# Value products of a half as one run, and norm roots on VectorE, in a two-layer hybrid encoder

## The chip, the cores and the metric

The kernel runs on one core of one Trainium2 chip. The metric is the device time of one execution in microseconds (us). Three executions of the kernel before took 1064.05 to 1065.41 us, with a median of 1065.24 us.

## The reference

The input is a sequence of 512 positions of 1024 channels (float32). Two layers follow each other. Each layer has a mixing part and a convolutional feed-forward part. Cut to what matters here, the mixing part is:

```python
h = rmsnorm(x, norm1[l]);  p = h @ w_in[l]          # columns: u (512) | q (8x64) | k (2x64) | v (2x64)
y_f = Re(fft2(u)) @ w_f + b_f                       # Fourier half
q = rope(rmsnorm(q, q_norm[l]))                     # each head of 64 is normed on its own
k = rope(rmsnorm(k, k_norm[l]))
# windowed attention: queries in 4 blocks of 128, keys of the own block and its two neighbours,
# |i - j| <= 128, a learned sink logit per head; 4 query heads share one key and value head
probs = softmax(concat([q @ k.T / 8, sink]))[..., :-1]
y_a = probs @ v
x = x + concat([rmsnorm(y_f), rmsnorm(y_a)]) @ w_o[l]
```

The feed-forward part is `x = x + (silu(g) * u) @ w_down` with `[g, u] = dwconv3(rmsnorm(x) @ w_up)`. It takes most of the time and is not touched by the change.

## The kernel before

Activations are kept transposed (channels on the partitions), and most products of float32 operands are made as three products of float32r parts: each operand is split into a rounded high part and a low rest (`split`, lines 98 to 105), and `mm3` (lines 114 to 122) accumulates high by high, low by high and high by low. A few products, the value products among them, are made on plain float32 operands; each of these is two MATMUL records in the trace.

A layer runs in these stages. The combined projection is made first for the columns of k, v and one pair of q heads, then for the rest (lines 373 to 396). `fold_h` (line 400) makes the folded inputs of the Fourier half on VectorE and ScalarE. `prep` (line 429) squares q or k on ScalarE, sums each head on VectorE, takes the inverse root with `rsqrt` (line 206), and applies norm scale and rotary tables on VectorE; it is called for k with q pair 3 (16 roots a partition) and later for q pairs 0 to 2 (24 roots a partition). `turn_k` and `turn_q` transpose the results on TensorE. Then come the two Fourier stages (line 594), with attention of pair 3 written between them and of pair 0 behind them, the product with `w_f` (line 622), the attention of pairs 1 and 2, and the output projection: its Fourier half (line 669) first, which is the fill for the attention of pairs 1 and 2, and its attention half (line 676) after it.

`attention(p, ...)` (line 500) handles one pair of heads in two halves of two query blocks each. For each block and head it makes the scores (line 517, PSUM tag `sc`), adds the mask and takes the extremum on VectorE (line 521), the exponential on ScalarE (line 524), the division on GpSimd (line 526), the transposes of the weights on TensorE (line 529, PSUM tag `tp`), and a copy of them out of PSUM into the tile `pT` on ScalarE (line 531, in the trace ACT at line 90, `pT<-ps`). After both blocks and both heads of a half come its six value products (line 536): for three key blocks, head 0 writes partitions 0 to 63 and head 1 partitions 64 to 127 of the pair's one PSUM bank `py` (tag `av`). A product reads only its own head's copies, so head 0's can go before head 1's are there. When both halves are in, `py` is split and squared (lines 540 and 541) for the output projection and the norm.

`rsqrt` is used for the eight norms over channels too (`col_rstd`, line 213, 4 roots a partition). In all cases VectorE makes scale and epsilon (line 209) and GpSimd the power of -1/2 (line 210). The result of the call with q is needed by line 443 on VectorE.

The order of each engine's instructions is not the order of the text: a planner (`schedule_with_timeline_sim=True`) simulates the program and puts each engine's instructions in the order in which they come up, with its own costs and the dependencies that it knows. Engines then run their queues in that fixed order and wait for each other on semaphores. Written by hand is only `issue_after`: each group of the output projection's Fourier half comes behind a certain transpose of the attention (`steps`, lines 530 and 659).

Of the kernel before, what the change touches and what calls it, by code (L numbers as in the profile page):

```python
# [8 lines left out]
F32 = mybir.dt.float32  # L9
F32R = mybir.dt.float32r  # L10
I32 = mybir.dt.int32
AF = mybir.ActivationFunctionType
ALU = mybir.AluOpType
# [3 lines left out]
P = 128  # L17
# [7 lines left out]
NB = S // P  # L25
# [12 lines left out]
def encoder_kernel(tc, t):  # L38
# [7 lines left out]
    nc = tc.nc  # L46
    ctxs = []

    def pool(**kw):
        cm = tc.tile_pool(**kw)  # L50
        ctxs.append(cm)
        return cm.__enter__()
# [4 lines left out]
    sp = pool(name="small", bufs=2)  # L57
# [6 lines left out]
    def nm(s):  # L64
        uid[0] += 1
        return f"{s}_{uid[0]}"
# [9 lines left out]
    def psum(tag="mm"):  # L76
        return ps.tile([P, 512], F32, tag=tag, name=nm("ps"), bufs=BANKS[tag])

    def temp(n, tag, dt=F32):
        size, bufs = TEMPS[tag]  # L80
        return tp.tile([P, size], dt, tag=tag, name=nm(tag), bufs=bufs)[:, :n]

    def pair(tag, n=512):
        return temp(2 * n, tag, F32R).rearrange("p (s q) -> p s q", s=2)
# [4 lines left out]
    def act(out, in_, func=AF.Copy, **kw):  # L89
        return nc.scalar.activation(out, in_, func, **kw)  # L90

    def tt(out, a, b, op, eng=None):
        return (eng or nc.vector).tensor_tensor(out, a, b, op=op)  # L93

    def stt(out, a, s, b, op0, op1):
        return nc.vector.scalar_tensor_tensor(out=out, in0=a, scalar=s, in1=b, op0=op0, op1=op1)  # L96

    def split(hi, lo, src, scale=None, eng=None):

        if scale is None:  # L100
            act(hi, src)
            tt(lo, src, f(hi), ALU.subtract, eng)
        else:
            act(hi, src, scale=scale)
            stt(lo, src, scale, f(hi), ALU.mult, ALU.subtract)
# [100 lines left out]
    def rsqrt(ssq, n, inv, tag, bufs=2):  # L206

        v, r = [sp.tile([P, n], F32, tag=tag + z, name=nm(tag + z), bufs=bufs) for z in "vr"]
        nc.vector.tensor_scalar(v, ssq, inv, EPS, op0=ALU.mult, op1=ALU.add)
        nc.gpsimd.tensor_tensor(r, v, mhalf[:, :1].to_broadcast([P, n]), op=ALU.pow)  # L210
        return r

    def col_rstd(acc, inv, tag="tp"):

        pt = psum(tag)
        for b in range(NB):
            nc.tensor.matmul(pt[:, 2 * b:2 * b + 2], acc[:, b * P:(b + 1) * P], ones2, start=True, stop=True)  # L217
        return rsqrt(pt[:, 0:2 * NB:2], NB, inv, "n")
# [51 lines left out]
    mhalf = cp.tile([P, 1], F32, tag="mhalf", name="mhalf")  # L270
# [40 lines left out]
    def add_square(acc, src, first, tag="sq"):  # L311
        if first:
            act(acc, src, AF.Square)
        else:
            sq = temp(512, tag)
            act(sq, src, AF.Square)
            tt(acc, acc, sq, ALU.add)
# [50 lines left out]
    for l in range(L):  # L368

        r1 = col_rstd(acc, 1.0 / D)  # L370
        vp = cp.tile([P, NB, P], F32, tag="v", name=nm("v"))
        qraw = {}
        for grp in (1, 0):
# [15 lines left out]
            n = 256 if grp else 384  # L389
# [39 lines left out]
        def prep(us):  # L429
# [5 lines left out]
            for i, u in enumerate(us):  # L435
                two = temp(1024, "act").rearrange("p (z b h d) -> p z b h d", z=2, **dims)
                act(two[:, 1], qraw[u], AF.Square)
                nc.vector.tensor_reduce(out=ssq[:, i], in_=two[:, 1], axis=AX.X, op=ALU.add)
                t12.append(two)
            r = rsqrt(ssq.rearrange("p n b h -> p (n b h)"), n * NB * 2, 1.0 / HD, f"qk{n}", 1)  # L440
            r = r.rearrange("p (n b h) -> p n b h", n=n, h=2)
            nr = sp.tile([P, n, NB, 2], F32, tag=f"qknr{n}", name=nm("qknr"), bufs=1)
# [54 lines left out]
        steps = []  # L497
        ya = {}

        def attention(p, first_pair):  # L500

            g = p // 2
            py = psum("av")
            stats = [[sp.tile([P, NB], F32, tag=f"{z}{e}", name=nm(z)) for z in ("nmax", "den")] for e in range(2)]
            pT = temp(2560, "pT").rearrange("p (z e b q) -> p z e b q", z=2, e=2, q=P)
            for half in range(2):
                for i in (2 * half, 2 * half + 1):
                    j0, j1 = max(0, i - 1), min(NB - 1, i + 1)
                    n = (j1 - j0 + 1) * P
                    m0 = P if i == 0 else 0  # L510
                    b0 = (0, 2, 0, 3)[i]
                    for e in range(2):
                        h = 2 * p + e
                        nmax, den = stats[e]
                        sc = psum("sc")
                        for s in range(2):
                            nc.tensor.matmul(sc[:, :n], qT[p][:, e, i * P:(i + 1) * P], kT[g][:, s, j0 * P:(j1 + 1) * P],  # L517
                                             start=s == 0, stop=s == 1)
                        pr = temp(385, "tA")
                        nc.gpsimd.tensor_copy(pr[:, n:n + 1], nsink[:, l, h:h + 1])  # L520
                        nc.vector.tensor_tensor_reduce(  # L521
                            out=pr[:, :n], in0=sc[:, :n], in1=mask[:, m0:m0 + n], scale=qs_scale[p][:, i, e:e + 1],
                            scalar=nsink[:, l, h:h + 1], op0=ALU.add, op1=ALU.min, accum_out=nmax[:, i:i + 1])
                        act(pr[:, :n + 1], pr[:, :n + 1], AF.Exp, scale=-1.0, bias=nmax[:, i:i + 1], accum_out=den[:, i:i + 1])
                        nc.vector.reciprocal(den[:, i:i + 1], den[:, i:i + 1])
                        nc.gpsimd.tensor_scalar(pr[:, :n], pr[:, :n], den[:, i:i + 1], 1.0, op0=ALU.mult, op1=ALU.mult)
                        pp = psum("tp")
                        for j in range(n // P):
                            tr = nc.tensor.transpose(pp[:, j * P:(j + 1) * P], pr[:, j * P:(j + 1) * P], ident)  # L529
                        steps.append(tr.ins)  # L530
                        act(pT[:, half, e, b0:b0 + n // P, :].rearrange("p b q -> p (b q)"), pp[:, :n])
                for j in ((0, 1, 2), (1, 2, 3))[half]:
                    i0, i1 = max(2 * half, j - 1), min(2 * half + 1, j + 1)
                    b0 = (0, 2, 0, 3)[i0] + j - max(0, i0 - 1)
                    for e in range(2):
                        nc.tensor.matmul(py[64 * e:64 * e + 64, i0 * P:(i1 + 1) * P], vp[:, j, 64 * g:64 * g + 64],  # L536
                                         pT[:, half, e, b0:b0 + 2 * (i1 - i0) + 1:2, :], start=(half, j) == (0, 0),
                                         stop=(half, j) == (1, 3), skip_group_check=True)
            ya[p] = pair("act")
            split(ya[p][:, 0, :], ya[p][:, 1, :], py, scale=gA[:, l, p:p + 1])  # L540
            add_square(accA, py, first_pair)
# [52 lines left out]
        for stage in range(2):  # L594
            pe = [psum(), psum(), psum("sc")]
            po = psum()
            for m in range(3):
                o = pe[m][:, :258]
                for i in range(2):
                    a, b = (ue, tabs) if stage == 0 else (tabs, ue)  # L600
                    mm3(o, [z[:, m * P:(m + 1) * P] for z in a[i]], [z[:, 0:258] for z in b[i]], i == 0, False)
                for z in ut:
                    if stage == 0:
                        c0 = (1, 1 + P, 0)[m]
                        nc.tensor.matmul(o, z[:, c0:c0 + P], alts, start=False, stop=z is ut[-1])
                    else:
                        nc.tensor.matmul(o, alts[:, :P], z, start=False, stop=z is ut[-1])
            for m in range(2):
                for i in range(2):
                    a, b = (ue, tabs) if stage == 0 else (tabs, ue)  # L610
                    mm3(po[:, m * 256:(m + 1) * 256], [z[:, 256 + m * P:384 + m * P] for z in a[i]],
                        [z[:, 256:512] for z in b[i]], m == 0 and i == 0, i == 1, skip_group_check=True)
            ue, ut = stage_out(pe, po, 1.0 if stage == 0 else 1.0 / 512.0)
            if stage == 0:
                for p, qs in enumerate(prep((0, 1, 2))):
                    qT[p] = turn_q(qs, "act")
                attention(3, True)
        attention(0, False)

        accF = accum("accF")  # L620
        yf = []
        for j in range(NF):
            pu = psum()
            pv = psum()
# [23 lines left out]
        for p in (1, 2):  # L648
            attention(p, False)
# [41 lines left out]
        for f0, nf in HALVES:  # L691
            gu = []
            for fi in range(f0, f0 + nf):
                ys_ = []
                n = fi - f0
# [30 lines left out]
            for m in range(KT):  # L726
# [3 lines left out]
                for c in range(0, nf, 8):  # L730
                    n = min(8, nf - c)
# [104 lines left out]
```

## Time and profile before

| | |
|---|---|
| Median of 3 executions | 1065.24 us |
| Profiled execution, its own time | 1065.23 us |
| Span of the profiled execution | 1063.4 us |
| TensorE (PE) busy | 1050.4 us |
| VectorE (DVE) busy | 722.4 us |
| ScalarE (ACT) busy | 507.7 us |
| GpSimd (POOL) busy | 115.6 us |

PE is TensorE's matmul part and PEld its weight loads, which overlap it. An instruction is named by line, engine, operation and the tiles it writes and reads (`ps<-pT,v`: into PSUM, from the weights and the values). A wait is put down to the instruction whose result came last. Matmuls are pipelined, so the duration of one is longer than the distance from its start to the next one's; what a matmul occupies is read from the starts.

### The profile page before, as it was taken

What the parts mean: (1) busy time and instruction counts of PE and PEld (TensorE: products, weight loads), DVE (VectorE), ACT (ScalarE), POOL (GpSimd) and SP (SyncE); (2) the same over time, 40 slices, a digit from 0 to 9 for tenths busy, and PEclk for the clock granted to TensorE, in tenths of its full rate; (3) what the DMA queues carried; (4) which work ended last, traced back from release to release, by engine and by line L of the source; (5) the groups of instructions that cost most, each with busy time, mean ns of one, the idle gap of its engine ahead of it and who ended that gap; (6) DMA issues with size and microseconds to landing.
All of it is one profiled execution on the core that took longest, in us unless ns stands there. A gap on an engine that the chain in (4) does not pass through costs nothing.

```text
span 1063.4 us, 14386 instructions
## 1 busy us (share of the span) xinstructions
PE 1050.4 (99%) x5107; PEld 876.5 (82%) x5107; DVE 722.4 (68%) x1340; ACT 507.7 (48%) x939; POOL 115.6 (11%) x168
## 2 busy tenths in 40 slices
PE   8999999999999999999999999999999999999998
PEld 7986778888888888888899877788888888888887
DVE  7868668697766777777519665387887336877632
ACT  5348755455443454455423875155554224544421
POOL 0134410000000000000001542001201000101100
PEclk9999999999999999999999999999999999999999
DMA  8233062233269932339857222422332333232241
GB/s 280 73 109 104 19 197 91 87 99 99 87 206 340 356 96 90 94 112 323 281 182 229 82 78 80 139 82 96 100 99 82 102 114 99 82 104 92 82 148 48
DMA packets 60475, 140.03 MB, mean 132 GB/s; under 512 B 6642, under 2 KB 22258, under 8 KB 60404
## 3 DMA queue, kind: packets, MB, share of 16 engines
q1 hardware_dynamic: 60404, 139.12, 40.3%
q8 instruction: 40, 0.66, 0.2%
q14 instruction: 31, 0.25, 0.1%
HBM read 116.02 MB, written 23.07 MB: 131 GB/s over the span
## 4 chain that ended last, share of the span: by engine, by line
PE 92%; DVE 4%; ACT 1%; POOL 1%; DMA 1%; issue 1%; SPq 0%; DVEq 0%; ACTq 0%; POOLq 0%
PE ps L120 27%; PE ps L121 27%; PE ps L122 27%; PE ps L118 3%; PE ps L536 3%; PE ps L529 2%; PE ps L517 2%; POOL qk3r L210 1%; PE ps L224 1%; DVE act L93 1%; PE ps L217 1%; DVE tF L96 1%; DVE tF L93 0%; DVE slab L93 0%; ACT tA L90 0%
## 5 line engine op out<-in xcount | busy, mean ns | idle before, releaser
L90 ACT ACTIVATE whi<-wraw 128x512 fp32r<-128x512 f32 (+1 forms) x296 | 181.8, 616 | 292.3 <-PE ps L122 275.2
L120 PE MATMUL ps<-act,whi 128*128 128x512 f32 x768 | 298.9, 390 | 0.0
L121 PE MATMUL ps<-act,wlo 128*128 128x512 f32 x768 | 298.7, 389 | 0.0
L122 PE MATMUL ps<-act,whi 128*128 128x512 f32 x768 | 298.4, 389 | 0.0
L93 DVE TENSOR_TENSOR wlo<-wraw,whi 128x512 fp32r<-128x512 f32 (+1 forms) x304 | 219.4, 724 | 100.5 <-ACT whi L90 99.1
L121 PEld LDWEIGHTS ps<-act,wlo 128*128 128x128 f32 x768 | 144.2, 188 | 29.9
L120 PEld LDWEIGHTS ps<-act,whi 128*128 128x128 f32 x768 | 144.2, 188 | 29.9
L122 PEld LDWEIGHTS ps<-act,whi 128*128 128x128 f32 x768 | 144.2, 188 | 29.7
L96 DVE SCALAR_TENSOR_TENSOR tF<-tF,pb,tF 128x511 f32<-128x511 f32 x176 | 133.2, 763 | 10.9 <-ACT tF L90 8.4
L93 DVE TENSOR_TENSOR tF<-ps,rb 128x512 f32<-128x512 f32 x104 | 71.1, 688 | 76.0 <-PE ps L122 64.3
L120 PE MATMUL ps<-slab,whi 128*128 128x512 f32 (+2 forms) x212 | 81.7, 386 | 0.0
L121 PE MATMUL ps<-slab,wlo 128*128 128x512 f32 (+2 forms) x212 | 80.2, 379 | 0.0
L122 PE MATMUL ps<-slab,whi 128*128 128x512 f32 (+2 forms) x212 | 80.0, 382 | 0.0
L90 ACT ACTIVATE tF<-tF,pb 128x512 f32<-128x512 f32 x88 | 71.5, 815 | 9.2 <-DVE tF L93 2.8
L93 DVE TENSOR_TENSOR x<-x,ps 128x512 f32<-128x512 f32 (+1 forms) x49 | 32.9, 673 | 41.0 <-PE ps L122 40.8
L93 POOL TENSOR_TENSOR tF<-tF,tF 128x512 f32<-128x512 f32 x22 | 30.4, 1384 | 255.9 <-DVE tF L96 224.1
L520 POOL COPY tA<-nsink 128x1 f32<-128x1 f32 x64 | 13.4, 216 | 362.3 <-DMA wraw<-in_w_down_dram 317.9
L521 DVE CUSTOM_DVE_ANT_0 tA<-ps,pb,nsink 128x256 f32<-128x256 f32 (+1 forms) x64 | 38.3, 605 | 20.1 <-PE ps L517 15.4
L120 PE MATMUL ps<-pT,whi 128*128 128x512 f32 (+1 forms) x132 | 50.5, 383 | 0.0
L121 PE MATMUL ps<-pT,wlo 128*128 128x512 f32 (+1 forms) x132 | 50.5, 383 | 0.0
L122 PE MATMUL ps<-pT,whi 128*128 128x512 f32 (+1 forms) x132 | 50.5, 383 | 0.0
L122 PEld LDWEIGHTS ps<-slab,whi 128*128 128x128 f32 x212 | 39.6, 188 | 8.4 <-issue 1.2
(170 smaller groups left out, 1545.2 us busy)
## 6 DMA issues: line engine op xcount, KB each, us to landing
wraw<-in_w_up_dram SPq DMA_DIRECT2D x88, 512.0 KB, 3.5
wraw<-in_w_down_dram SPq DMA_DIRECT2D x32, 512.0 KB, 3.6
kept<-tA SPq DMA_DIRECT2D x56, 256.0 KB, 5.5
whi<-kept SPq DMA_DIRECT2D x28, 256.0 KB, 3.0
wlo<-kept SPq DMA_DIRECT2D x28, 256.0 KB, 3.2
kept<-tA SPq DMA_DIRECT2D x32, 192.0 KB, 1.9
wraw<-in_w_down_dram SPq DMA_DIRECT2D x32, 192.0 KB, 2.4
wraw<-in_w_o_dram SPq DMA_DIRECT2D x8, 512.0 KB, 4.1
```

What stands on the lines that cost most here:

```text
L90: return nc.scalar.activation(out, in_, func, **kw)
L93: return (eng or nc.vector).tensor_tensor(out, a, b, op=op)
L96: return nc.vector.scalar_tensor_tensor(out=out, in0=a, scalar=s, in1=b, op0=op0, op1=op1)
L118: nc.tensor.matmul(out, a[0], b[0], start=start, stop=stop, **kw)
L120: nc.tensor.matmul(out, a[0], b[0], start=start, stop=False, **kw)
L121: nc.tensor.matmul(out, a[1], b[0], start=False, stop=False, **kw)
L122: nc.tensor.matmul(out, a[0], b[1], start=False, stop=stop, **kw)
L517: nc.tensor.matmul(sc[:, :n], qT[p][:, e, i * P:(i + 1) * P], kT[g][:, s, j0 * P:(j1 + 1) * P], start=s == 0, stop=s == 1)
L520: nc.gpsimd.tensor_copy(pr[:, n:n + 1], nsink[:, l, h:h + 1])
L521: nc.vector.tensor_tensor_reduce(out=pr[:, :n], in0=sc[:, :n], in1=mask[:, m0:m0 + n], scale=qs_scale[p][:, i, e:e + 1], scalar=nsink[:, l ...
L529: tr = nc.tensor.transpose(pp[:, j * P:(j + 1) * P], pr[:, j * P:(j + 1) * P], ident)
L536: nc.tensor.matmul(py[64 * e:64 * e + 64, i0 * P:(i1 + 1) * P], vp[:, j, 64 * g:64 * g + 64], pT[:, half, e, b0:b0 + 2 * (i1 - i0) + 1:2, ...
```

## The change

All six value products of a half get a dependency on the last copy of the half into `pT`, which is head 1's. The new object `both_ready` says that it is a dependency on data, kept by a semaphore. In `rsqrt`, calls with more than four roots a partition no longer use GpSimd's power: VectorE makes a first guess from the bits of the number (two integer steps) and refines it in three rounds of three steps. Calls with four roots keep the power. The helpers `tt` and `stt` are one VectorE instruction each.

```diff
         nc.vector.tensor_scalar(v, ssq, inv, EPS, op0=ALU.mult, op1=ALU.add)
-        nc.gpsimd.tensor_tensor(r, v, mhalf[:, :1].to_broadcast([P, n]), op=ALU.pow)
+        if n <= NB:
+            nc.gpsimd.tensor_tensor(r, v, mhalf[:, :1].to_broadcast([P, n]), op=ALU.pow)
+            return r
+        q = sp.tile([P, n], F32, tag=tag + "q", name=nm(tag + "q"), bufs=bufs)
+        it = sp.tile([P, n], I32, tag=tag + "i", name=nm(tag + "i"), bufs=bufs)
+        nc.vector.tensor_scalar(it, v.bitcast(I32), 1, None, op0=ALU.logical_shift_right)
+        nc.vector.tensor_scalar(r.bitcast(I32), it, -1, float(0x5F3759DF), op0=ALU.mult, op1=ALU.add)
+        for _ in range(3):
+            tt(q, r, r, ALU.mult)
+            stt(q, q, -0.5, v, ALU.mult, ALU.mult)
+            stt(r, q, 1.5, r, ALU.add, ALU.mult)
         return r
...
+        both_ready = mybir.DependencyInfo(mybir.DependencyClass.Sync, mybir.DependencyReason.DATA)
+
         def attention(p, first_pair):
...
-                        act(pT[:, half, e, b0:b0 + n // P, :].rearrange("p b q -> p (b q)"), pp[:, :n])
+                        ready = act(pT[:, half, e, b0:b0 + n // P, :].rearrange("p b q -> p (b q)"), pp[:, :n])
                 for j in ((0, 1, 2), (1, 2, 3))[half]:
...
                     for e in range(2):
-                        nc.tensor.matmul(py[64 * e:64 * e + 64, i0 * P:(i1 + 1) * P], vp[:, j, 64 * g:64 * g + 64],
+                        pv = nc.tensor.matmul(py[64 * e:64 * e + 64, i0 * P:(i1 + 1) * P], vp[:, j, 64 * g:64 * g + 64],
                                          pT[:, half, e, b0:b0 + 2 * (i1 - i0) + 1:2, :], start=(half, j) == (0, 0),
                                          stop=(half, j) == (1, 3), skip_group_check=True)
+
+                        tc.add_manual_dep(pv.ins, ready.ins.name, both_ready, reason="paired values")
```

## Rows read from the trace of the kernel before

**Rows 1.** Page: TensorE's busy time, share and instructions; the chain by engine.
```profile
PE 1050.4 (99%) x5107; PEld 876.5 (82%) x5107; DVE 722.4 (68%) x1340; ACT 507.7 (48%) x939; POOL 115.6 (11%) x168
...
PE 92%; DVE 4%; ACT 1%; POOL 1%; DMA 1%; issue 1%; SPq 0%; DVEq 0%; ACTq 0%; POOLq 0%
```

**Rows 2.** Busy time of each engine by stage (PE, PEld, DVE, ACT, POOL; instructions).
```profile
79.00:117.00 38.00, 36.00 (x221) 26.22 (x219) 29.31 (x98) 33.20 (x92) 17.44 (x39) 1.00 0.24 73
117.00:157.00 40.00, 39.71 (x208) 29.17 (x207) 27.91 (x67) 24.00 (x59) 9.27 (x21) 1.00 0.44 142
558.00:586.00 28.00, 28.00 (x194) 28.00 (x193) 27.77 (x67) 10.11 (x19) 5.22 (x2) 1.00 0.72 235
...
602.00:641.00 39.00, 38.74 (x280) 31.23 (x280) 26.81 (x95) 31.92 (x95) 16.80 (x47) 1.00 0.17 55
641.00:678.00 37.00, 37.00 (x178) 26.60 (x177) 15.57 (x40) 12.07 (x32) 7.04 (x13) 1.00 0.36 115
```

**Rows 3.** TensorE in order of time, pair 2 of layer 1: start, us, instruction, count.
```profile
657.75 0.65 PE L536 MATMUL ps<-pT,v 128*64 128x256 f32 x2
658.33 0.55 PE L529 MATMUL ps<-ident,tA 128*128 128x128 f32 x3
...
659.50 1.30 PE L536 MATMUL ps<-pT,v 128*64 128x256 f32 x10
660.73 0.55 PE L529 MATMUL ps<-ident,tA 128*128 128x128 f32 x3
...
662.12 0.43 PE L536 MATMUL ps<-pT,v 128*64 128x128 f32 x2
662.48 0.50 PE L120 MATMUL ps<-slab,whi 128*128 128x512 f32 x1
...
669.00 0.39 PE L120 MATMUL ps<-slab,whi 128*128 128x512 f32 x1
669.32 1.08 PE L536 MATMUL ps<-pT,v 128*64 128x256 f32 x6
670.33 0.50 PE L121 MATMUL ps<-slab,wlo 128*128 128x512 f32 x1
670.67 0.40 PE L122 MATMUL ps<-slab,whi 128*128 128x512 f32 x1
670.90 0.39 PE L120 MATMUL ps<-slab,whi 128*128 128x512 f32 x1
```

**Rows 4.** The same view: the first run of line 536, and runs of a whole half.
```profile
91.37 0.65 PE L536 MATMUL ps<-pT,v 128*64 128x256 f32 x2
...
138.61 1.51 PE L536 MATMUL ps<-pT,v 128*64 128x256 f32 x14
140.05 0.55 PE L529 MATMUL ps<-ident,tA 128*128 128x128 f32 x3
...
638.84 1.30 PE L536 MATMUL ps<-pT,v 128*64 128x256 f32 x12
640.07 0.77 PE L529 MATMUL ps<-ident,tA 128*128 128x128 f32 x5
```

**Rows 5.** GpSimd's power (ns), VectorE's waits at line 443, line 209 in order of time.
```profile
L210 POOL TENSOR_TENSOR qk3r<-qk3v,mhalf x2: 9361/9388/9414, 57.6 to 584.1; 128x24 f32<-128x24 f32 x2
...
DVE qknr L443 <- POOL qk3r L210: 5.9, 2, 3.4
...
568.27 0.16 DVE L209 TENSOR_SCALAR qk2v<-qkssq 128x16 f32<-128x16 f32 x1
568.35 0.75 DVE L93 TENSOR_TENSOR act<-pT,ropetab 128x256 f32<-128x256 f32 x2
```

**Rows 6.** TensorE's waits (us, times, longest); ScalarE's copies out of PSUM by form.
```profile
PE ps L605 <- DVE tail L96: 1.2, 1, 1.2
...
PEld ps L536 <- ACT pT L90: 1.9, 6, 0.4
...
L90 ACT ACTIVATE pT<-ps 128x384 f32<-128x384 f32 x32 | 15.6, 497 | 6.3 <-PE ps L529 6.1
```

## The prediction

> **What bounds the kernel now.** I read the page first: TensorE is busy for 1050.4 of 1063.4 us, and the chain that ended last lies 92% on it [rows 1]. So what counts is TensorE's occupancy, and another engine only where it lets TensorE stand. Next I read the busy times by stage [rows 2]. The value products (line 536) fall into four stages: 79 to 117 us and 602 to 641 us (pairs 3 and 0 of layers 0 and 1, beside the second Fourier stage), and 117 to 157 us and 641 to 678 us (pairs 1 and 2, beside the output projection's fill). In the two fill stages TensorE stands for 0.3 us of 77 while ScalarE has work for 60% and 33% of the time: occupancy saved there is time saved. In the other two ScalarE is busy for 33.2 of 38 us and 31.9 of 39 us, and in the first TensorE already stands for 2.0 us: occupancy saved there may partly come back as waiting. Last I read TensorE's instructions in order of time around line 536, since a group's mean does not tell how products follow each other [rows 3, 4].
>
> **Part one, the products of a half as one run.** One product is two matmul records. Where both heads' products follow each other they overlap: a run of twelve records, a whole half, starts at 638.84 and the next instruction at 640.07, 1.23 us [rows 4]. Where one head's product goes alone, it has the engine to itself: 256 columns 657.75 to 658.33, 0.58 us, and 128 columns 662.12 to 662.48, 0.36 us. The rest of a split first half, ten records, costs as much as the whole twelve: 659.50 to 660.73, 1.23 us. The rest of a split second half, six records, takes 669.32 to 670.33, 1.01 us [rows 3].
>
> Today's 16 halves stand in 42 runs, the first at 91.37 us [rows 4], the last at 669.32 [rows 3]. First halves: four of eight are split, as 0.58 + 1.23 = 1.81 us. Second halves: six go as 0.36 + 0.36 + 0.58 + 1.01 = 2.31 us, and two have their first product attached to the run of the half before (fourteen records, 138.61 to 140.05, 1.44 us [rows 4]). With every half as a run of 1.23 us:
> 4 x 0.58 = 2.3; 6 x 1.08 = 6.5; 2 x (1.44 + 0.36 + 0.58 + 1.01 - 2 x 1.23) = 1.9; together 10.7 us.
>
> A run also costs at its two ends. In the fill one matmul follows another by 0.23 us (670.67 to 670.90), but the last before the run of 669.32 takes 0.32 and the first after it 0.34 [rows 3]: 0.09 + 0.11 = 0.20 us. Behind a score matmul or ahead of a transpose it is less; over the 42 runs I read 0.13 us from the starts. 26 fewer runs x 0.13 = 3.4 us (between 26 x 0.06 = 1.6 and 26 x 0.20 = 5.2). In all 14.1 us of TensorE's time.
>
> What of it is on the path, by stage. Fill stages: 1.9 us (pairs 1 and 2 of layer 0) and 1.08 + 0.58 + 1.08 = 2.7 us (layer 1), and 11 runs fewer x 0.13 = 1.4: 6.0 us, taken whole, since the fill goes on behind the last run (rows 3 end in it). The other two stages hold 14.1 - 6.0 = 8.1 us. I take half, 4.0 us: there the early head's product was also what TensorE did while ScalarE copied out the late head's weights. Taking 0 or 8.1 gives the ends. Sum: -10.0 us.
>
> The added wait holds TensorE's queue: behind a half's first product stand the next transposes, scores and fill, in their fixed order. The last product of a half ends hardly later than before, because it needed the late head's copy already: the run behind that copy grows by 0 in the first half (1.23 for 1.23) and by 0.22 us in the second (1.23 for 1.01). The PSUM bank of the pair is read by ScalarE after it, off the path while fill is left.
>
> **Part two, the roots.** GpSimd loses two powers a layer, the one for 24 columns 9.4 us long. VectorE's queue stood at the instruction behind it, line 443, for 5.9 us in two times [rows 5]. VectorE gains 11 small steps a root, 44 in all. The nearest row is line 209's scale and add, on 16 columns: 0.16 us long, with the next, independent instruction 0.08 us behind its start [rows 5]. A chain that waits for each result costs at least the 0.16. So a root takes 0.9 to 1.8 us of VectorE's queue, 1.8 to 3.6 a layer, against 2.9 us of standing a layer that go.
>
> The Trainium skill, "VectorE: DVE Perf Modes", section "The DRAIN you can't avoid", has it that the next operation on VectorE starts only when the pipe has emptied, whether there is a semaphore or not, so that one should keep the number of operations low. By that rule a root would take the upper of the two figures in any case; the trace does not bear it out for an independent successor, which starts at half of line 209's duration, and the sum goes by the rows.
>
> Who waits: in layer 0 nobody that the rows show. In layer 1 TensorE stood 1.2 us for the tail's low half, which VectorE gave behind line 443 [rows 6]; that should go. Against it, VectorE is busy for 27.8 of the 28 us from 558 to 586 [rows 2], and the folded inputs that TensorE takes from 574 on come out of that same queue: the key root's steps stand among them and could hold TensorE by up to the 3.6 us. I take 0 for part two, between -1.2 and +3.6: the gain and the likely loss are of one size.
>
> The profiled execution took 1065.23 us (a span of 1063.4 and 1.8 around it), as good as the median of the runs, 1065.24. 1065.2 - 10.0 = 1055.2; I say 1055.
>
> **Rivals.** (A) All comes back: the stages beside the Fourier work are also bound by TensorE, and the tail's wait goes: 1065.2 - 14.1 - 1.2 = 1049.9. For it: TensorE stands for only 0.3 of the 39 us from 602 to 641 [rows 2]. Against it: ScalarE's load there.
>
> (B) Only the fill stages give: 1065.2 - 6.0 = 1059.2, with 1063 as its end if part two costs its 3.6. For it: from 79 to 117 us ScalarE is busy for 87% of the time, and TensorE waits there already.
>
> (C) No difference: the instructions of every engine are put in order by a planner, and with 16 new waits and 44 new instructions it finds another order over the whole attention. If it does not put the six together, or puts a stall elsewhere that eats 10 us, the time is 1063.1 to 1067.4. For it: VectorE's standing behind the power, 5.9 us, shows that the plan and the chip can differ by microseconds. Against it: four halves go out whole in today's order already.
>
> (D) Slower: the wait is exposed at TensorE's head in every half. Between the late head's last transpose and its product lie the transpose's own end (three in a row span 0.55 us at 658.33 [rows 3]; 0.3 for the last is my estimate from it), ScalarE's copy of 0.50 us for 384 columns, and any copy queued ahead of it on ScalarE (another 0.5) [rows 6]: 0.8 to 1.3 us x 16 = 12.8 to 20.8 us. From 14.1 / 16 = 0.88 us a half it eats the whole gain, from 1.01 us the kernel is slower by more than 0.2%; with one copy ahead, 1.3 us, it comes to 1065.2 - 14.1 + 20.8 = 1071.9. For it: nothing of the early head is left to fill that gap. Against it: line 536's weight loads waited for this copy six times in all, 1.9 us and never over 0.4 [rows 6], and there is other work to put there.
>
> The Trainium skill, "TensorE: Matmul & The Clock Gate", section "Part 3: Packing small matmuls — row/col tiling", says that matmuls start and end strictly in program order; by it nothing could slip past a held run, which is what (D) needs. The starts in the rows read here are in such an order, but none of them shows a run held for long.
>
> **How the numbers follow.** Forecast (1052 to 1058.5) 0.50; A (below 1052) 0.12; B (1058.5 to 1063.1) 0.20; C 0.09; D 0.09. 0.2%, 2.1 us, is about what a measurement of this kernel can tell from no change. So faster 0.82, same 0.09, slower 0.09. The range leaves out D, most of C and the lowest third of A: 1050 to 1063.5; the forecast's own is 1052 to 1058.5.
>
> **What would show it.** Right: 16 runs of line 536 with twelve records each and some 1.23 us apart from what follows; TensorE's busy time lower by 8 us or more, and the projection's fill over earlier by about that in each layer; GpSimd without the powers of 16 and 24 columns; no wait of VectorE at line 443. Wrong: more than 0.4 us of waiting for ScalarE's copy ahead of most runs (D); runs still in pieces (C); TensorE's idle time between 79 and 117 us grown by what its runs lost (B); a wait of TensorE for the folded inputs after 574 us, of 1 us or more, which would be part two's loss.

## The result, and the profile after

The changed kernel takes 1056.75 us (median of 4 executions, 1055.7 to 1057.71) against 1065.18 us of the kernel before in the same comparison: a ratio of 0.992, with a 95% interval of 0.991 to 0.994. That is 8.4 us less; 10 were forecast. The profiled execution took 1056.14 us, with a span of 1054.3.

The page of the changed kernel, TensorE's busy time and the chain by engine, as in [rows 1]:

```profile
PE 1038.2 (98%) x5107; PEld 873.2 (83%) x5107; DVE 726.8 (69%) x1384; ACT 507.9 (48%) x939; POOL 90.8 (9%) x164
...
PE 93%; DVE 2%; DMA 2%; ACT 1%; issue 1%; POOL 0%; SPq 0%; ACTq 0%; DVEq 0%; POOLq 0%
```

TensorE is busy for 12.2 us less with the same 5107 instructions, and it stands for 16.1 us in place of 13.0. The stages of [rows 2], at the same places of the span:

```profile
79.00:117.00 38.00, 34.74 (x229) 27.22 (x229) 30.29 (x100) 36.23 (x98) 18.68 (x43) 1.00 0.22 71
117.00:157.00 40.00, 39.44 (x218) 30.94 (x219) 27.49 (x67) 22.69 (x57) 8.29 (x17) 1.00 0.48 155
558.00:586.00 28.00, 28.00 (x203) 27.86 (x203) 26.21 (x78) 10.23 (x21) 0.00 (x0) 1.00 0.84 273
...
602.00:641.00 39.00, 36.47 (x261) 29.92 (x262) 28.73 (x97) 32.23 (x92) 20.74 (x47) 1.00 0.16 50
641.00:678.00 37.00, 37.00 (x210) 29.52 (x207) 12.87 (x32) 10.65 (x27) 4.97 (x11) 1.00 0.46 156
```

The new idle time is where the Fourier work runs beside the attention: 3.3 us from 79 to 117 (2.0 before) and 2.5 us from 602 to 641 (0.3 before). In the fill stages it is 0.6 us of 77 (0.3 before). TensorE in order of time around pair 2 of layer 1, which answers to [rows 3] (line 536 is now 548, and 529 is 541):

```profile
651.82 0.40 PE L122 MATMUL ps<-slab,whi 128*128 128x512 f32 x1
652.14 1.30 PE L548 MATMUL ps<-pT,v 128*64 128x256 f32 x12
653.38 0.55 PE L541 MATMUL ps<-ident,tA 128*128 128x128 f32 x3
...
660.14 0.39 PE L122 MATMUL ps<-slab,whi 128*128 128x512 f32 x1
660.46 1.30 PE L548 MATMUL ps<-pT,v 128*64 128x128 f32 x12
661.69 0.50 PE L120 MATMUL ps<-slab,whi 128*128 128x512 f32 x1
```

Each half is one run of twelve records and 1.23 us (660.46 to 661.69), in all 16 cases. What takes the place of [rows 6] among TensorE's waits (us in total, times, longest):

```profile
PEld ps L541 <- POOL tA L538: 3.7, 8, 1.3
...
PEld ps L548 <- ACT tA L90: 1.0, 3, 0.4
...
PE ps L541 <- ACT act L90: 1.4, 2, 1.1
```

The runs hardly wait: no row of line 548 waits for ScalarE's copy `pT`, and the wait for VectorE's tail (line 605 before) is gone. The largest sum is at the transposes of the attention (line 541), which waited before the change too (line 529):

```profile
PEld ps L529 <- POOL tA L526: 2.8, 7, 0.7
```

What is new ahead of the attention is the root of the keys. VectorE in order of time in layer 1, from the key root's scale and add (line 209) to the use of the root (line 453):

```profile
563.65 0.17 DVE L209 TENSOR_SCALAR qk2v<-qkssq 128x16 f32<-128x16 f32 x1
563.73 0.76 DVE L93 TENSOR_TENSOR act<-pT,ropetab 128x256 f32<-128x256 f32 x2
564.40 0.17 DVE L341 COPY tF<-tF 128x2 f32<-128x2 f32 x1
564.47 0.69 DVE L93 TENSOR_TENSOR slab<-tF,slab 128x512 fp32r<-128x512 f32 x1
565.07 0.17 DVE L215 TENSOR_SCALAR qk2i<-qk2v 128x16 int32<-128x16 int32 x1
565.15 0.75 DVE L93 TENSOR_TENSOR tF<-tF 128x255 f32<-128x255 f32 x2
565.82 0.74 DVE L96 SCALAR_TENSOR_TENSOR tF<-x,pa,rb 128x512 f32<-128x512 f32 x1
566.48 0.68 DVE L93 TENSOR_TENSOR act<-act 128x512 f32<-128x512 f32 x1
567.09 0.17 DVE L216 TENSOR_SCALAR qk2r<-qk2i 128x16 int32<-128x16 int32 x1
...
571.98 0.17 DVE L96 SCALAR_TENSOR_TENSOR qk2r<-qk2q,qk2r 128x16 f32<-128x16 f32 x1
...
583.27 0.43 DVE L96 SCALAR_TENSOR_TENSOR slab<-ps,slab 128x257 fp32r<-128x257 f32 x1 [1.79 <-ACT slab L90]
...
585.06 0.17 DVE L453 TENSOR_SCALAR qknr<-qk2r 128x16 f32<-128x16 f32 x1
```

A step is 0.17 us long, but the next step of the chain comes only after one, two or more of the long operations queued between them: 1.4 us from line 209 to 215, 2.0 from 215 to 216, and 21.4 us for the whole root. In this are 1.8 us in which VectorE stood: the last steps are queued behind an instruction that waits for ScalarE's copy of a Fourier result (583.27).

### The profile page after: what moved, and what is told of

The parts are those of the page before. It is cut to its first block, busy times and chain, and to the rows that moved or that the text cites. A ratio compares the mean times of both kernels' runs of the same rounds, so it can differ in the third digit from the quotient of the medians.

```text
span 1054.3 us, 14425 instructions
## 1 busy us (share of the span) xinstructions
PE 1038.2 (98%) x5107; PEld 873.2 (83%) x5107; DVE 726.8 (69%) x1384; ACT 507.9 (48%) x939; POOL 90.8 (9%) x164
## 4 chain that ended last, share of the span: by engine, by line
PE 93%; DVE 2%; DMA 2%; ACT 1%; issue 1%; POOL 0%; SPq 0%; ACTq 0%; DVEq 0%; POOLq 0%
PE ps L122 28%; PE ps L120 28%; PE ps L121 28%; PE ps L118 3%; PE ps L548 2%; PE ps L541 2%; PE ps L529 1%; DMA wraw<-in_w_qkv_dram 1%; PE ps L234 1%; PE ps L227 1%; ACT tA L90 0%; DMA x<-in_xT_dram 0%; DVE tA L533 0%; ACT act L90 0%; PE ps L500 0%
## 5 line engine op out<-in xcount | busy, mean ns | idle before, releaser
L538 POOL TENSOR_SCALAR tA<-tA,den 128x256 f32<-128x256 f32 (+1 forms) x64 | 37.4, 590 | 145.1 <-DVE den L537 144.6
```

## The experiments

All were timed beside the kernel before on the same chip, whose median was 1065.88 us in the first comparison (first four kernels), 1065.53 in the second (six rounds, key power, one round, pair run with power) and 1065.32 in the third (the last three). "Gain" is the difference of the medians within one comparison; the changed kernel's is 8.4 us.

For the place of a gain I compare two intervals of the profiled executions, by TensorE's starts. In layer 0 it runs from the first plain Fourier product (line 118) to the norm behind the attention (the first matmul of `col_rstd`), in layer 1 from the broadcast of the layer's first norm (`row_rstd`) to the same norm. In the kernel before they are 111.2 and 121.8 us long. Two pairs of kernels below that share the form of a layer agree in it within 0.02 us. For the changed kernel and for key power (below) the ends of the second interval are:

```profile
551.72 1.05 PE L234 MATMUL ps<-ident,nr 128*128 128x128 f32 x8
...
669.33 0.84 PE L227 MATMUL ps<-ones,acc 128*128 128x2 f32 x7
```

```profile
551.26 1.05 PE L234 MATMUL ps<-ident,nr 128*128 128x128 f32 x8
...
664.73 0.95 PE L227 MATMUL ps<-ones,acc 128*128 128x2 f32 x8
```

That is 117.6 and 113.5 us.

**The products alone.** The edit to the changed kernel:

```diff
-        if n <= NB:
-            nc.gpsimd.tensor_tensor(r, v, mhalf[:, :1].to_broadcast([P, n]), op=ALU.pow)
-            return r
...
-            stt(r, q, 1.5, r, ALU.add, ALU.mult)
+        nc.gpsimd.tensor_tensor(r, v, mhalf[:, :1].to_broadcast([P, n]), op=ALU.pow)
```

> Part one alone: the products of a half wait for both heads, the roots stay with GpSimd's power. Theory (the gain is TensorE time given back by the products, the roots are worth nothing): 1055 to 1059 us, 16 runs of twelve records, VectorE again standing at line 443 for 5 to 6 us. Rival (a good part of the gain comes from the roots, because VectorE no longer stands behind the power): 1060 to 1064 us.

Measured: 1053.35 us, a ratio of 0.988 (0.987 to 0.990), a gain of 12.5 us. That is 1.7 us below the theory's range: the products are worth more than the whole change.

**The roots alone.** The diff of `rsqrt` in the kernel before, nothing else.

> Part two alone: the roots as VectorE steps, the products wait for their own head only. Theory: 1063 to 1067 us, the products again in some 40 runs. Rival (the roots carry the gain): 1057 to 1062 us.

Measured: 1070.81 us, 1.0044 (1.0031 to 1.0056), a loss of 4.9 us. Both the theory (no effect) and the rival (the roots carry the gain) fall: the roots cost time. The two parts add, 12.5 - 4.9 = 7.6 us against 8.4 together. The page's first line of each, the products alone and then the roots alone:

```profile
PE 1036.4 (99%) x5107; PEld 874.1 (83%) x5107; DVE 721.2 (69%) x1340; ACT 506.0 (48%) x939; POOL 115.8 (11%) x168
```

```profile
PE 1053.9 (99%) x5107; PEld 878.2 (82%) x5107; DVE 726.9 (68%) x1384; ACT 509.1 (48%) x939; POOL 92.2 (9%) x164
```

From [rows 1] the products take 14.0 us off TensorE's busy time, the sum that was worked out (14.1), and 12.5 of them come back as time.

**Heads in turn.** Inside a run the three products of head 0 stand ahead of those of head 1:

```diff
-                for j in ((0, 1, 2), (1, 2, 3))[half]:
...
-                    for e in range(2):
+                for e in range(2):
+                    for j in ((0, 1, 2), (1, 2, 3))[half]:
```

> The changed kernel, but with the three products of head 0 ahead of the three of head 1 inside each run: still one run a half, but neighbours write the same half of the partitions. Theory (two heads' products side by side share the engine's time, and that is most of the gain): a run grows from 1.23 to some 2.3 us (two records of 256 columns 0.43, of 128 columns 0.22, six products 2.16), 16 x 1.07 = 17 us, of which the idle time of the attention may swallow a few: 1066 to 1074 us. Rival (the gain is in the fewer ends of runs, not in the overlap): 1056 to 1060 us.

Measured: 1061.74 us, 0.996 (0.995 to 0.997), a gain of 4.1 us, half of the changed kernel's. Its runs of pair 2 of layer 1, with what follows them:

```profile
657.28 1.78 PE L548 MATMUL ps<-pT,v 128*64 128x256 f32 x12
659.00 0.55 PE L541 MATMUL ps<-ident,tA 128*128 128x128 f32 x3
...
666.11 1.57 PE L548 MATMUL ps<-pT,v 128*64 128x128 f32 x12
667.61 0.50 PE L120 MATMUL ps<-slab,whi 128*128 128x512 f32 x1
```

A first half takes 1.72 us and a second 1.50, not 2.3, because the edit takes away little of the overlap. By the records' starts only head 0's first product goes alone: head 1's first record starts at 657.771, 6 ns behind the first record of head 0's second product and ahead of that product's second record (657.981), and from there the heads run side by side. The kernel's text has all of head 0's records first; whether the planner or the engine lets head 1 in earlier, the trace does not tell. So the growth is 8 x 0.49 + 8 x 0.27 = 6.1 us in place of 17. By the medians 4.3 of it are time (8.4 - 4.1), by the two intervals 2.5 + 2.8 = 5.3. The direction is the theory's, its size was not. With the number of runs unchanged, the overlap of one product in three is worth this much; the rival, that only the ends of the runs count, falls. How the gain is shared between overlap and ends, this run does not show.

**One run for a pair.** The product loops stand behind both halves, and all twelve products wait for the pair's last copy:

```diff
+            for half in range(2):
                 for j in ((0, 1, 2), (1, 2, 3))[half]:
```

> The changed kernel, but all twelve products of a pair wait for the pair's last copy: 8 runs of 24 records in place of 16 of twelve. Theory: 8 fewer runs x 0.13 us = 1 us less of TensorE's time and nothing else late: 1054.5 to 1057 us. Rival (the work kept back is missed where TensorE has to wait, from 79 to 117 us and 602 to 641 us): 1058 to 1062 us.

Measured: 1055.39 us, 0.990 (0.989 to 0.991), a gain of 10.5 us. A run of 24 records, the last pair's:

```profile
658.17 2.38 PE L549 MATMUL ps<-pT,v 128*64 128x256 f32 x24
660.49 0.50 PE L120 MATMUL ps<-slab,whi 128*128 128x512 f32 x1
```

It takes 2.32 us where two of twelve took 2.46, and one pair of ends is saved. By the medians that is 2.1 us better than the changed kernel, by the intervals 1.2: 1.5 better in layer 0 and 0.3 worse in layer 1. There the rival (work missed elsewhere) shows: TensorE stands for 3.6 us from 602 to 641 in place of 2.5.

**Why the roots cost: rounds.** Twice as many rounds, and one:

```diff
-        for _ in range(3):
+        for _ in range(6):
```

> The changed kernel with six rounds of refinement a root in place of three: 20 steps in place of 11 (one suspected cost nearly doubled). Theory (what part two costs is the lateness of the key root: each of its dependent steps stands behind an operation of 0.4 to 1.3 us in VectorE's queue, 21 us in all in the changed kernel against 5 to 8 us with the power): the key root takes 30 us or more, the key transposes come later, 1059 to 1064 us. Rival (the cost is VectorE's time for the steps themselves): 36 steps more x 0.08 us = 2.9 us in all, mostly hidden: 1056.5 to 1058.5 us.

> The changed kernel with one round of refinement: 5 steps a root in place of 11; this leaves out two rounds of the roots' accuracy. Theory (lateness by the length of the dependent chain): the key root takes some 10 us in place of 21, 1053.5 to 1055.5 us. Rival (VectorE's time): 24 steps less x 0.08 us = 1.9 us, mostly hidden: 1056 to 1057 us.

Measured: six rounds 1058.39 us, 0.993 (0.992 to 0.994), a gain of 7.1 us; one round 1054.13 us, 0.989 (0.988 to 0.991), a gain of 11.4 us. One round takes the time that the theory had, but its key root takes 19.0 us in layer 0 and 10.9 in layer 1, not some 10 in both. Six rounds do not come out as the theory had it: by the medians they are not told apart from three, within the rival's range. The first rows of each pair below are line 209 for the keys, the second the use of the root (durations in ns, first and last start in us: layer 0 and layer 1); six rounds, then one round:

```profile
L209 DVE TENSOR_SCALAR qk2v<-qkssq x2: 161/164/168, 43.6 to 565.1; 128x16 f32<-128x16 f32 x2
...
L453 DVE TENSOR_SCALAR qknr<-qk2r x2: 167/167/167, 69.0 to 590.1; 128x16 f32<-128x16 f32 x2
```

```profile
L209 DVE TENSOR_SCALAR qk2v<-qkssq x2: 161/164/166, 43.4 to 562.1; 128x16 f32<-128x16 f32 x2
...
L453 DVE TENSOR_SCALAR qknr<-qk2r x2: 149/157/165, 62.4 to 573.0; 128x16 f32<-128x16 f32 x2
```

The nine more steps make the key root only 3.6 us later (25.0 and 25.4 us against 21.4 and 21.9 with three rounds): when they come up, VectorE's queue has few long operations left to put between them. So the number of steps is not what counts, but what stands between them.

**The same steps without the lateness.** The power gives the root again, and VectorE does all 11 steps into a tile that nothing reads:

```diff
+        rr = sp.tile([P, n], F32, tag=tag + "w", name=nm(tag + "w"), bufs=bufs)
+        nc.gpsimd.tensor_tensor(rr, v, mhalf[:, :1].to_broadcast([P, n]), op=ALU.pow)
...
-        return r
+        return rr
```

> The changed kernel, whose roots are taken from GpSimd's power again while VectorE does all of its steps too, into a tile that nothing reads: the same work on VectorE without the lateness. Theory (lateness of the key root): 1052.5 to 1054.5 us, like the products' part alone (1053.35 us). Rival (VectorE's time for the steps, and what they displace in its queue): 1056 to 1058 us.

Measured: 1053.73 us, 0.989 (0.988 to 0.991), a gain of 11.6 us, not told apart from the products alone. The key root in this kernel, and below it in the products alone:

```profile
L209 DVE TENSOR_SCALAR qk2v<-qkssq x2: 166/166/167, 43.6 to 564.5; 128x16 f32<-128x16 f32 x2
...
L455 DVE TENSOR_SCALAR qknr<-qk2w x2: 158/160/163, 51.7 to 569.5; 128x16 f32<-128x16 f32 x2
```

```profile
L209 DVE TENSOR_SCALAR qk2v<-qkssq x2: 170/170/170, 43.6 to 563.3; 128x16 f32<-128x16 f32 x2
...
L443 DVE TENSOR_SCALAR qknr<-qk2r x2: 161/164/166, 52.0 to 568.1; 128x16 f32<-128x16 f32 x2
```

With VectorE's work kept and the root used after 8.1 and 5.0 us, the cost is gone. It was the lateness: the changed kernel does the same steps on VectorE and waits for their result, and by the intervals that costs it 0.5 us in layer 0 and 3.9 in layer 1.

**Which root.** Only the key root goes back to the power:

```diff
-        if n <= NB:
+        if n <= 4 * NB:
```

> The changed kernel with the key root (16 roots a partition) back on GpSimd's power and only the 24 roots of the queries as VectorE steps. Theory (the key root's lateness is the whole cost): 1052.5 to 1054.5 us, as good as the products' part alone or a little better, since VectorE no longer stands behind the long power. Rival (the query root's steps cost as much as the key root's): 1055 to 1057 us.

Measured: 1052.43 us, 0.988 (0.986 to 0.989), a gain of 13.1 us. The key root was the cost; the queries' root may stay on VectorE. Against the products alone (0.987 to 0.990) the difference is not clear. The intervals show where the lateness costs (us; the key root from line 209 to its use):

| Kernel | Key root, layer 0 | Interval, layer 0 | Key root, layer 1 | Interval, layer 1 |
|---|---|---|---|---|
| before | 8.4 | 111.2 | 4.8 | 121.8 |
| roots alone | 23.4 | 114.3 | 21.4 | 124.8 |
| products alone | 8.4 | 106.9 | 4.8 | 115.1 |
| key power | 8.4 | 108.1 | 4.8 | 113.5 |
| power and steps | 8.1 | 108.0 | 4.9 | 113.7 |
| one round | 19.0 | 107.4 | 10.9 | 115.7 |
| changed kernel | 21.9 | 108.6 | 21.4 | 117.6 |
| six rounds | 25.4 | 108.6 | 25.0 | 118.5 |

From key power down (one and six rounds change the queries' root as well), in layer 1 the time rises with the key root, by 5.0 us from the shortest to the longest. In layer 0 it does not: a root that is 13 us later costs 0.5 us there, and the one of 19.0 us stands in the shortest interval. The attention's starts agree: against key power the first scores of the changed kernel start 5.5 us later in layer 1, counted from the interval's start, and only 0.9 us later in layer 0. The queries' root on VectorE costs 1.2 us in layer 0 and gains 1.7 in layer 1 (key power against the products alone), which the medians do not show.

TensorE's idle time agrees for layer 1. It falls from 2.5 us between 602 and 641 to 1.4 and 1.3 with the key root early, and from 79 to 117 it does not fall (3.3 us; 3.5 and 3.3). Key power, then power and steps:

```profile
79.00:117.00 38.00, 34.51 (x228) 27.02 (x228) 30.71 (x102) 35.86 (x98) 18.42 (x43) 1.00 0.23 71
602.00:641.00 39.00, 37.56 (x272) 31.34 (x270) 28.20 (x93) 29.37 (x85) 17.93 (x45) 1.00 0.22 68
```

```profile
79.00:117.00 38.00, 34.75 (x231) 27.34 (x231) 29.54 (x97) 35.87 (x98) 18.19 (x43) 1.00 0.24 74
602.00:641.00 39.00, 37.70 (x282) 31.10 (x283) 28.09 (x98) 31.06 (x92) 20.93 (x49) 1.00 0.19 56
```

**Two ways to put the parts together.** First the run of a pair with all roots on the power:

> All twelve products of a pair as one run, and all roots on GpSimd's power. Theory (the two effects add: 12.5 us gained by the products' part alone, 1.4 us more by runs of a whole pair): 1051 to 1053 us. Rival (with the roots early the attention is no longer late, and the run of a whole pair gives nothing more): 1053 to 1055 us.

Measured: 1053.41 us, 0.989 (0.987 to 0.990), a gain of 12.1 us. The rival has the number: in all, the run of a pair adds nothing to the products alone. Its reason is not shown, for the profile reads differently by layer: against the products alone the interval of layer 0 is 2.0 us shorter and that of layer 1 is 1.6 us longer. Layer 0's interval was 6.3 us shorter than before with it and 3.1 with the key root on the power; layer 1's was 5.1 us shorter with it and 8.4 with the key root on the power. So each layer got its better form:

```diff
-        if n <= NB:
+        if n <= NB or power:
...
+                    if half < (0 if l else 1) or (l and vh != half):
+                        continue
...
+            r = rsqrt(..., power=l == 0 or n == 2)
```

> The best of each layer in the profiles so far, put together: in layer 0 all twelve products of a pair as one run and both roots on GpSimd's power; in layer 1 runs of a half, the key root on the power and the query root as VectorE steps. Theory (the layers add): 1050 to 1051.5 us. Rival (what one layer gains is lost by a plan that comes out another way): 1052 to 1054 us.

Measured: 1049.76 us (1049.72 to 1049.95), 0.985 (0.984 to 0.987), a gain of 15.6 us, below the theory's range by 0.2 us. It beats the changed kernel by 7 us, and its intervals, 104.9 and 113.5 us, are those of the two forms that it was put together from: the layers add. Its page's first line:

```profile
PE 1034.8 (99%) x5107; PEld 874.1 (83%) x5107; DVE 722.6 (69%) x1351; ACT 505.7 (48%) x939; POOL 106.7 (10%) x167
```

**Second halves only.** From the products alone:

```diff
-                        tc.add_manual_dep(pv.ins, ready.ins.name, both_ready, reason="paired values")
+                        if half == 1:
+                            tc.add_manual_dep(pv.ins, ready.ins.name, both_ready, reason="paired values")
```

> The products' part alone, and only the products of a pair's second half wait for both heads. Theory (gain by the runs that are spared): the second halves stood in 30 of the 42 runs; 8.4 us by the prices of single products and 22 fewer runs x 0.13 = 2.9 us, 11.3 of the 14.1 us that all halves give. With the 89% of it that the products' part alone gave back (12.5 of 14.1): 10 us, 1054.5 to 1057 us. Rival (the gain comes by the plan, not by the runs): no such proportion, 1058 us or more, or no worse than 1053.5.

Measured: 1055.05 us, 0.990 (0.989 to 0.992), a gain of 10.3 us. All second halves go out as one run; four of the eight first halves stay split, as before. The gain follows the number and price of the runs.

## Why the prediction was right, and where its terms were off

*The price of the runs* was right: 14.1 us were worked out from six rows of the kernel before, and the products alone take 14.0 us off TensorE's busy time. The share of the second halves, as it was worked out ahead of that run, was right too (10 us expected, 10.3 measured).

*How much of it is on the path* was set too low. I took 6.0 us of the fill stages whole and half of the other 8.1; the products alone gain 12.5 us. If the fill gave its 6.0, about 6.5 of the 8.1 came through. By the starts the fill gave a little less: cut at the broadcast of the Fourier norm, and with the few matmuls that changed sides set right, I estimate some 7 us ahead of it and some 5 behind it. So both kinds of stage gave about the same share, and to halve the one was the mistake. The cover that I feared for, the early head's product while ScalarE copies for the late one, was hardly needed: no run of line 548 waited for that copy in the changed kernel. In the products alone one matmul did, 0.4 us, and six weight loads, 1.9 us in all and 0.6 at most, about as in [rows 6]. That also settles rival (D): the planner had other work to put there in nearly all 16 places.

*Part two* is the term that was mis-sized: taken as 0, between -1.2 and +3.6, it measures +4.9 us alone and +4.1 beside the products (12.5 - 8.4), outside its own bounds. Its named gains came: VectorE stands behind no power any more, and TensorE's wait for the tail is gone. The step that failed is the price of a root. I gave it 0.9 to 1.8 us as occupancy of VectorE's queue, by the distance of one step to the next instruction, and looked for the damage in the folded inputs. There TensorE waited for VectorE for 0.3 us. But a chain of 11 steps, each of which needs the one before, in a queue that is busy for 27.8 of 28 us [rows 2], is not 11 x 0.08 us long: it takes as long as all that the plan puts between its steps, 21 us. The keys came out of it 13 us later than by the power in layer 0, and some 16 us in layer 1. In layer 1 the attention behind them came later too, by 5.5 us, and there the time was lost; in layer 0 little of it was.

The rule of the Trainium skill that I weighed against that row, "VectorE: DVE Perf Modes", section "The DRAIN you can't avoid", says that the next operation waits until the pipe is empty, but it adds that one which is not held back starts earlier. I left that out: by the section the upper figure, 1.8 us a root, does not hold in every case. The traces agree with the addition where the successor is independent (563.65 to 563.73, 0.08 us, behind a step of 0.17). It would not have helped either way: neither figure is the one that mattered.

The two errors have opposite signs, +2.5 and -4.1 us, which is why the sum of 10 came within 1.6 us of the measured 8.4. That is luck. Rival (B), only the fill stages give, would have been within 2.5 us of the time too, for the wrong reason.

What stays open: the products free 14.0 us of TensorE's busy time, and 12.5 us are gained; TensorE's idle time grows by 2.2 us of span in the products alone (13.0 to 15.2). From 79 to 117 and from 602 to 641 us it grows by 1.8 us, in the fill of layer 0 (117 to 157) by 0.7. Which of the planner's choices costs it was not tried. How the lateness of the keys turns into 4 us of time is known by its place, the attention of layer 1, but not in every step. Of the 4.1 us that key power saves in that interval, only 1.6 are idle time of TensorE. The other 2.6 stand in the same 771 matmul records, which the trace counts as busy: by their starts the 80 transposes of line 541 take 8.3 us there and 7.1 with the key root early. The waits put down to line 541 do not tell the two apart: its weight loads wait for line 538 for 3.7 us in the changed kernel and for 4.6 us with key power.

## What to carry to other kernels

Where two heads' products with 64 output partitions each can overlap, let both wait for the later head: a product that goes alone costs its full time and two ends of a run, and on a busy TensorE nearly all of what is saved comes back. Before moving a small serial computation onto a busy engine, price it as a chain: its length in steps times the distance between two free places in that queue, not the sum of its durations. Then ask whether what needs the result is on the path: much the same lateness cost 4 us in one layer and 0.5 us in the other. A slow instruction on an idle engine can be the better place, and one test settles it: do the work on the busy engine as well, but take the result from the idle one.

## What the runs showed of the hardware that was not expected

GpSimd's power on the same shape does not always take the same time. It takes 1.02 us for 4 columns and 3.35 us for 16. For 24 columns it took 9.4 us in the kernel before, but 5.8 and 6.2 us in power and steps:

```profile
L210 POOL TENSOR_TENSOR nr<-nv,mhalf x8: 1006/1017/1028, 25.6 to 717.5; 128x4 f32<-128x4 f32 x8
L210 POOL TENSOR_TENSOR qk2r<-qk2v,mhalf x2: 3347/3348/3350, 43.7 to 568.5; 128x16 f32<-128x16 f32 x2
...
L214 POOL TENSOR_TENSOR qk3w<-qk3v,mhalf x2: 5823/5992/6160, 59.3 to 580.8; 128x24 f32<-128x24 f32 x2
```

The first two rows are from the kernel before, the third from power and steps. What makes the difference was not tried.

A run of 24 value products' records takes 0.14 us less than two of twelve, beside the ends.

The first 45 us differ between executions, and TensorE's granted clock differs with them. In the profile of the kernel before it was at its lower level, 1.2 GHz, for some 3.4 us; in the changed kernel's it was at 2.4 GHz there. Just ahead of it TensorE had stood for GpSimd's power, 2.1 us in the first and 1.5 us in the second. Before, then after:

```profile
27.30:30.60 3.30, 3.30 (x14) 3.30 (x13) 0.85 (x2) 2.42 (x8) 0.00 (x0) 0.50 0.00 1
```

```profile
27.30:30.60 3.30, 3.30 (x23) 3.30 (x23) 0.58 (x1) 2.68 (x9) 0.00 (x0) 1.00 0.02 9
```

The eight profiles with such a stretch start the first plain Fourier product at 46.2 to 46.8 us, the five without it at 44.5 to 45.5. It is at 46.2 before and at 44.9 in the changed kernel's profile, so 1.3 us of the 9.1 between the two spans are not the change's. Timed executions of one kernel differ in this as well: the changed kernel took 1055.70 us at a mean granted clock of 1.000 and 1057.36 and 1057.71 at 0.998. So a difference of 1.5 us between two medians can come from this alone. The intervals above lie behind this stretch.
